# Opening of a fused encoder step: the first direct tiles and the sink column

## The chip, the cores and the metric

The kernel runs on one core of a Trainium2 chip, as one program and one launch. The metric is device time in microseconds, the median of several runs. The core has five engines that work side by side, each through its own queue in order: TensorE (PE; PEld is its weight load), VectorE (DVE), ScalarE (ACT), GpSimd (POOL) and SyncE (SP), whose queue issues nearly all transfers (DMA).

## The reference

One post-norm layer of a streaming encoder over 2048 prompt tokens and 8 x 16 sample tokens, in float32:

```python
qm, km, vm, om, ip, fp, qa, ka, va = split_in(x @ w_in)     # D_MODEL 1024 -> 2824
hm = og * head_norm(mlstm_chunkwise(qm, km, vm, logi, logf, ...))   # 4 heads x 128
qa, ka = rope(qa, pos), rope(ka, pos)
ha = band_attend(qa, ka, va, mask, attn_sinks)              # 8 q heads, 2 kv heads x 64
h = layer_norm(ALPHA * x + concat(hm, ha) @ w_out)
y = layer_norm(ALPHA * h + conv_ffn(h))                     # up 5632, causal conv of 3, silu gate, down
```

The attention's softmax has a learned sink for each head: `p = exp(s - mx) / (sum exp(s - mx) + exp(sink - mx))`, where `mx` is the maximum of the scores and the sink.

## The kernel before

Every float32 operand of a large product is split into a rounded high half (`S.copy` into float32r on ScalarE, L217 for weights, L565 for activations) and a low half (a subtraction on VectorE, L218 and L566); a product is then three matmuls, high-high, high-low and low-high.

The input projection (`i_dense`) goes over four blocks of tokens (`IBLOCKS`): block 0 holds prompt tiles 0 to 3 and the sample tile 16, the others four tiles each; a tile is 128 tokens. Five groups of 512 output columns (`NG`) are computed by a Strassen-like scheme with seven products for each group: an activation block is cut into four quarters, q = 1 to 4 (features halves 0 and 1, by token halves 0 and 1: q 1 is tiles 0 and 1 with the first half of the features, q 2 tiles 2 and 3 with the first, q 3 and q 4 the same with the second), and `x_steps` makes the sums ("t1" to "t4") and the splits (1, 2, 3, 4, 5, 6, 7 and "b12") that the products s = 1 to 7 read. `split_first` makes the sums of the weights on the way.

The gate and key/value columns (264 of them) do not go through that scheme. They are "direct" products (`i_direct`, L730): 8 slices of 128 features, three matmuls each, so 24 for a tile. Their weights come in four pieces of 264 KB (`wg`), their activations from the same splits: tiles 0 and 1 read the splits 1 (first half of the features) and 2 (second half), tiles 2 and 3 read "b12" and 3. Behind each, `i_keys` evicts the result (L738, L739 on ScalarE), turns the keys by rope (four operations on VectorE, L868 to L871) and stores them.

The order of TensorE's work is written out by hand in `i_begin`, as a list of items ("t", block, tile, ...) for directs and ("p", block, group, s) for products; `manual_schedule` keeps it. The other engines' queues are put in order by the framework's scheduler from the program and its priorities. Before the change the list begins with the directs of tiles 2 and 3, then product 1 of group 0, the direct of the sample tile, and the other products; the directs of tiles 0 and 1 stand behind block 0's last product, in front of those of tiles 2 and 3 of block 1. `advance` prefetches weights as far as free slots allow (four raw slots, eight split halves).

Beside this dense work run "chains" (`Chains`): the sample tile, the mLSTM and the attention, which are woven between the dense matmuls once `i_done` says that a block is complete. After the direct of tile 1 a counter of six items starts (`after = [6, b + 1]`); `gate_logs` then makes the logarithms of the gates on VectorE and ScalarE, and the chains may begin.

In the attention (`swa`, `scores`) the scores of four heads go into a tile `sc` with one more column, the sink. The sink column is written by GpSimd (L1297) at the beginning of `scores`; VectorE writes the masked scores and their maximum (L1307, L1310); `exps` (L1315, ScalarE) exponentiates both together with a running sum. `sc` has two buffers.

During blocks 2 and 3 `d_sums` makes sums of the down-projection's weights on VectorE (tiles `txy`, L850 to L853).

Of the kernel before, what the change touches and what calls it, by code (L numbers as in the profile page):

```python
# [204 lines left out]
class Prog:  # L205
# [131 lines left out]
    def i_begin(self):  # L337
        self.ib = [self.dps.tile([P, 512], F32, name="dps", tag="dps") for _ in range(3)]
        it = []
        nb = len(IBLOCKS)  # L340
        for b in range(nb):
            if b == 0:
                it += [("t", 0, i, -1) for i in (2, 3)]

                it += [("p", 0, 0, 1), ("t", 0, 4, -1), ("p", 0, 0, 2), ("p", 0, 1, 1), ("p", 0, 0, 7), ("p", 0, 0, 6)]
            else:
                it += [("p", b, 0, s) for s in (1, 7, 6, 2)]
            for g in range(NG):
                if b == 0:

                    it += [("p", b, g, s) for s in (6, 2)] * (g > 0) + [("p", b, g, 5)]
                    if g + 1 < NG:
                        it += [("p", b, g + 1, 1)] * (g > 0) + [("p", b, g, 4), ("p", b, g, 3), ("p", b, g + 1, 7)]
                    else:
                        it += [("p", b, g, 3), ("p", b, g, 4)]
                elif g + 1 < NG:

                    it += [("p", b, g, s) for s in (6, 7, 2)] * (g > 0)
                    it += [("p", b, g, 5), ("p", b, g + 1, 1), ("p", b, g, 3), ("p", b, g, 4)]
                else:  # L360
                    it += [("p", b, g, s) for s in (6, 7, 5, 2, 3, 4)]
            it += [("t", b, i, b) for i in (0, 1)]
            if b + 1 < nb:
                it += [("t", b + 1, i, b) for i in (2, 3)]
        self.items = it

        uq = []
        for i in it:
            if i[0] == "p":
                uq.append(i)  # L370
            elif ("g", i[3], 0) not in uq:
                uq += [("g", i[3], u) for u in range(4)]
        uq += [("o", b, h, u) for b in range(len(OBLOCKS)) for h in range(2) for u in range(4)]
        self.uq = uq
        self.wu, self.hx, self.xr = {}, {}, {}
        self.us = self.ur = 0

        self.halves = [0, 0]
        self.raws = []
        self.raw_of = {}  # L380
        self.xn = self.ny = 0
        self.hs = {}
        self.spare = False
        self.extra, self.ring, self.turn = None, 2 * WB, 0
        self.raws.append([None, False])
# [148 lines left out]
    def x_load(self, b, *qs):  # L534
        for q in qs:
            self.xr[b, q] = r = self.x_raw(q)
            self.nc.sync.dma_start(r, self.a["xq"][b][(q - 1) // 2, (q - 1) % 2])

    def x_steps(self, b, *steps):

        nc, V = self.nc, self.nc.vector
        r = lambda q: self.xr[b, q]
        for s in steps:
            if s == "t3":
                self.spare = False
                self.xt = e = self.raw_slot([P, 4, HT]) if b else [self.tp.tile([P, 4, HT], F32, name="xt", tag="qk", bufs=2), False]
                V.tensor_sub(e[0], r(4), r(2))
            elif s == "t2":

                V.tensor_add(self.xt[0], self.xt[0], r(1))  # L550
            elif s == "t4":

                V.tensor_sub(r(4), r(3), self.xt[0])
                self.xt[1] = True
            elif s == "t1":

                V.tensor_sub(r(2), r(2), r(1))
            else:
                x = self.xt[0] if s in (7, 6) else r({1: 1, 2: 3, 3: 4, "b12": 2, 5: 2, 4: 4}[s])

                self.hx[b, s] = h, l = self.x_slot(4 if s == "b12" else s)
                n = 4 if (b, s) == (0, "b12") else 1
                for i in range(n):
                    k = slice(i * 4 // n, (i + 1) * 4 // n)
                    nc.scalar.copy(h[:, k], x[:, k])  # L565
                    V.tensor_sub(l[:, k], x[:, k], h[:, k].bitcast(F32))  # L566
# [20 lines left out]
    def i_dense(self):  # L587
# [2 lines left out]
        last = NG - 1  # L590

        self.next_raw()
        self.x_load(0, 2)
        for _ in range(3):
            self.next_raw()
        self.x_load(0, 4)
        self.single_raw = self.tp.tile([P, KD, P], F32, name="xsr", tag="pth", bufs=2)
        nc.sync.dma_start(self.single_raw, a["xs"])
        self.angles = {}
        self.rope_load(IBLOCKS[0][2], 2)  # L600
        self.rope_load(NPT, 1)
        self.next_split()
        self.x_steps(0, "b12")
        for _ in range(3):
            self.next_split()
        self.x_steps(0, 3)
        self.x_single(1, 2)
        self.x_load(0, 1)
        self.next_raw()
        self.x_load(0, 3)  # L610
        self.x_steps(0, 1)
        self.advance()
        self.x_steps(0, 2, "t3", 7, "t2", 6)
        self.x_single(4)
        self.x_steps(0, "t1", 5, "t4")
        self.sb, self.trans = {}, None
# [5 lines left out]
        for item in self.items:  # L622
# [9 lines left out]
            if item[0] == "t":  # L632
                _, b, ti, e = item
                if ("g", e, 3) not in self.wu:
                    self.advance()
                if b not in self.gates:
                    self.gates[b] = self.tp.tile([P, 5, 8], F32, name="gates", tag="gates", bufs=2)
                ps = self.bank([P, 512], "pg") if ti == 4 else self.ib[ti % 2 * 2]
                yield from self.i_direct(b, ti, e, ps)
                self.i_keys(b, ti, ps)  # L640
                if ti == 1:
                    if b + 1 < nb:
                        self.x_steps(b + 1, 1, 2)
                    else:
                        self.release(4)
                    after = [6, b + 1]
                elif ti == 3 and b or ti == 4:
                    self.release(4)
                    self.x_steps(b, 4)
                    if b:  # L650
                        self.x_steps(b, 5)
                self.advance()
                continue
# [9 lines left out]
                behind = self.i_after(b, g, s)  # L663
            if (b, g, s) == (0, 0, 7):
                self.t_setup()
            if (g, s) == (1, 6):
                self.rope_load(IBLOCKS[b][0], 2)
            if g == last and b + 1 < nb:
                if s == 7:
# [45 lines left out]
                if k % 2:  # L715
                    yield 645

    def i_direct(self, b, ti, e, ps):

        mm = self.nc.tensor.matmul  # L720
        for k in range(KD):
            wh, wl = [w[:, k % 2] for w in self.wu["g", e, k // 2]]
            if ti == 4:
                xh, xl = [self.hs[1 if k < 4 else 2][:, i, k % 4] for i in range(2)]
# [546 lines left out]
    def swa(self, t):  # L1271
# [19 lines left out]
        def scores(j0):  # L1291
# [2 lines left out]
            sc = self.work("sc", [P, 4, 2 * P + 4], bufs=2)  # L1294
            mx, sm = [self.work(n, [P, 4], bufs=2) for n in ("amx", "asm")]
            w = lambda x: x.rearrange("p (k j) -> p k j", k=2)
            nc.gpsimd.tensor_copy(sc[:, :, N:N + 1].rearrange("p (k j) o -> p k (j o)", k=2), sink)  # L1297
            ps = [self.bank([P, 2, 2, P], "psc") for _ in range(2)]
            for j in range(2):
                for i, (q, k) in enumerate(((qh, self.kh), (qh, self.kl), (ql, self.kh))):  # L1300
# [7 lines left out]
                                           op0=ALU.add, op1=ALU.max, accum_out=mx[:, c:c + 1])  # L1308

            V.scalar_tensor_tensor(w(mx), w(mx), -0.125, nsink, op0=ALU.mult, op1=ALU.min)  # L1310
            return sc, mx, sm

        def exps(sc, mx, sm):
# [872 lines left out]
```

## Time and profile before

| | |
|---|---|
| runs | 2315.28, 2317.24, 2321.0 us; median 2317.24 |
| profiled execution | 2316.15 us, of which the span is 2314.3 |
| mean granted TensorE clock | 0.996 |
| TensorE busy | 2281.9 us (99%) |
| VectorE, ScalarE, GpSimd busy | 1808.1 (78%), 1269.0 (55%), 279.5 us (12%) |
| moved | 632.38 MB, mean 273 GB/s |

The rows of the profile read as follows. A row of the timeline has start, length, engine, line, operation, output and input tiles with their shapes, how often in a row, and in brackets the idle time of the engine just before, with what ended it. A row of stages has the stage, its length, the busy time of PE, PEld, DVE, ACT and POOL with counts, the granted clock, the mean busy share of the 16 DMA engines and GB/s. A row of waits has who waited for whom, the total, how often, and the longest. Lines are those of the kernel before.

### The profile page before, as it was taken

What the parts mean: (1) busy time and instruction counts of PE and PEld (TensorE: products, weight loads), DVE (VectorE), ACT (ScalarE), POOL (GpSimd) and SP (SyncE); (2) the same over time, 40 slices, a digit from 0 to 9 for tenths busy, and PEclk for the clock granted to TensorE, in tenths of its full rate; (3) what the DMA queues carried; (4) which work ended last, traced back from release to release, by engine and by line L of the source; (5) the groups of instructions that cost most, each with busy time, mean ns of one, the idle gap of its engine ahead of it and who ended that gap; (6) DMA issues with size and microseconds to landing.
All of it is one profiled execution on the core that took longest, in us unless ns stands there. A gap on an engine that the chain in (4) does not pass through costs nothing.

```text
span 2314.3 us, 39788 instructions
## 1 busy us (share of the span) xinstructions
PE 2281.9 (99%) x14293; PEld 2094.9 (91%) x14293; DVE 1808.1 (78%) x3075; ACT 1269.0 (55%) x2377; POOL 279.5 (12%) x509
## 2 busy tenths in 40 slices
PE   8999999999999999999999999999999999999998
PEld 8999989989877778999999999999999978888876
DVE  8777687787688888998788777678766786895987
ACT  5453466776766655555656555555555544444442
POOL 0001000000011212121002000013111200100200
PEclk9999999999999999999999999999999999999999
DMA  7888999999977757888778889978898776756743
GB/s 276 287 308 297 301 309 336 314 310 342 315 269 240 240 201 270 303 319 311 276 289 274 306 304 311 315 264 287 312 294 261 225 282 208 261 175 215 255 157 108
DMA packets 300166, 632.38 MB, mean 273 GB/s; under 512 B 47869, under 2 KB 141121, under 8 KB 299969
## 3 DMA queue, kind: packets, MB, share of 16 engines
q1 hardware_dynamic: 295296, 616.14, 77.9%
q0 software_dynamic: 3520, 10.56, 1.4%
q10 hardware_dynamic: 1152, 3.15, 0.4%
q8 instruction: 113, 1.85, 0.3%
q14 instruction: 85, 0.69, 0.1%
HBM read 458.11 MB, written 171.64 MB: 272 GB/s over the span
## 4 chain that ended last, share of the span: by engine, by line
PE 76%; DVE 5%; DMA 4%; issue 2%; ACT 1%; SPq 0%; POOL 0%; DVEq 0%; ACTq 0%; POOLq 0%
PE dps L1873 19%; PE fup L1873 19%; PE dps L704 7%; PE dps L2083 6%; PE fht L2083 6%; PE fup L2083 6%; PE dps L222 2%; PE dps L224 2%; PE dps L223 2%; PE ppo L1348 1%; PE psc L1303 1%; PE ppt L1342 1%; DVE w L218 1%; PE fht L1697 1%; DMA txy<-wdn 0%
## 5 line engine op out<-in xcount | busy, mean ns | idle before, releaser
L1873 PE MATMUL dps<-hh,uw 128*128 128x384 f32 (+1 forms) x1848 | 478.7, 328 | 2.0 <-DVE u L1904 2.0
L1873 PE MATMUL fup<-hh,uw 128*128 128x384 f32 (+1 forms) x1848 | 478.2, 328 | 1.5 <-ACT ua L1894 1.5
L1873 PEld LDWEIGHTS dps<-hh,uw 128*128 128x128 f32 x1848 | 330.5, 188 | 2.2 <-DVE u L1904 2.2
L1873 PEld LDWEIGHTS fup<-hh,uw 128*128 128x128 f32 x1848 | 330.0, 188 | 2.0 <-ACT ua L1894 1.9
L1930 DVE SCALAR_TENSOR_TENSOR cc<-u,cw,cc 128x768 f32<-128x768 f32 (+1 forms) x264 | 258.1, 978 | 64.9 <-ACT cc L1928 55.5
L1873 PE MATMUL fup<-hl,uw 128*128 128x384 f32 (+1 forms) x924 | 302.5, 327 | 1.7 <-DVE hl L218 1.7
L1873 PE MATMUL dps<-hl,uw 128*128 128x384 f32 (+1 forms) x924 | 302.8, 328 | 0.0
L704 PE MATMUL dps<-w,oh 128*128 128x256 f32 x1344 | 254.3, 284 | 0.7 <-DVE zev L777 0.7
L217 ACT CAST uw<-wraw 128x1024 fp32r<-128x1024 f32 x126 | 123.0, 979 | 223.8 <-PE dps L2083 120.1
L218 DVE TENSOR_TENSOR w<-wraw,w 128x1024 fp32r<-128x1024 f32 (+2 forms) x167 | 189.4, 1141 | 56.1 <-ACT w L217 48.9
L217 ACT CAST w<-wraw 128x1024 fp32r<-128x1024 f32 (+2 forms) x167 | 163.0, 985 | 107.3 <-PE dps L704 38.9
L704 PEld LDWEIGHTS dps<-w,oh 128*128 128x128 f32 x1344 | 210.5, 188 | 11.8 <-issue 8.1
L218 DVE TENSOR_TENSOR uw<-wraw,uw 128x1024 fp32r<-128x1024 f32 x126 | 142.4, 1131 | 65.7 <-ACT uw L217 65.5
L704 PE MATMUL dps<-w,ol 128*128 128x256 f32 x672 | 187.8, 279 | 0.0
L704 PE MATMUL dps<-oh,w 128*128 128x256 f32 x896 | 170.9, 285 | 6.6 <-ACT mr L1153 3.8
L1873 PEld LDWEIGHTS fup<-hl,uw 128*128 128x128 f32 x924 | 173.5, 188 | 2.4 <-DVE hl L218 2.3
L2083 PE MATMUL fup<-uw,fu 128*128 128x512 f32 x726 | 174.2, 396 | 0.6 <-DVE uw L218 0.6
L1873 PEld LDWEIGHTS dps<-hl,uw 128*128 128x128 f32 x924 | 173.8, 188 | 0.0
L2083 PEld LDWEIGHTS fup<-uw,fu 128*128 128x128 f32 x726 | 136.6, 188 | 34.1 <-DVE uw L218 1.1
L2083 PE MATMUL dps<-uw,fu 128*128 128x512 f32 x660 | 165.3, 396 | 1.1 <-DVE uw L218 1.1
L1928 ACT ACTIVATE cc<-u,cw 128x768 f32<-128x768 f32 (+1 forms) x132 | 132.2, 1002 | 57.8 <-DVE u L1910 28.5
L704 PEld LDWEIGHTS dps<-oh,w 128*128 128x128 f32 x896 | 142.2, 191 | 13.1 <-ACT mr L1153 4.1
(318 smaller groups left out, 4567.0 us busy)
## 6 DMA issues: line engine op xcount, KB each, us to landing
uw<-zw SPq DMA_DIRECT2D x176, 512.0 KB, 5.1
zw<-uw SPq DMA_DIRECT2D x88, 512.0 KB, 3.7
w<-zws SPq DMA_DIRECT2D x72, 512.0 KB, 6.2
wv<-wup SPq DMA_DIRECT2D x66, 512.0 KB, 5.0
wraw<-wi SPq DMA_DIRECT2D x65, 512.0 KB, 5.1
wraw<-zt SPq DMA_DIRECT2D x60, 512.0 KB, 4.3
wraw<-wdn SPq DMA_DIRECT2D x45, 512.0 KB, 4.3
wraw<-wo SPq DMA_DIRECT2D x40, 512.0 KB, 4.5
```

What stands on the lines that cost most here:

```text
L217: nc.scalar.copy(hi, src)
L218: nc.vector.tensor_sub(lo, src, hi.bitcast(F32))
L222: mm(out, ah, bh, start=start, stop=False)
L223: mm(out, ah, bl, start=False, stop=False)
L224: mm(out, al, bh, start=False, stop=stop)
L704: mm(o, l, r, start=s in (1, 7) and c == k == i == 0, stop=k == 3 and i == 2, skip_group_check=True)
L1303: nc.tensor.matmul(ps[kvh][:, j, :nk], q[rs, j0 + j], k[rs, sel], start=i == 0, stop=i == 2)
L1342: nc.tensor.transpose(pp[:, j * P:(j + 1) * P], scs[j // 2][:, 2 * kvh + j % 2, kt * P:(kt + 1) * P], self.ident)
L1873: mm(ps, l[:, k], r[:, k], start=s in (1, 7) and k == 0 and i == 0, stop=k == 3 and i == 2, skip_group_check=True)
L1928: S.activation(c[:, v], u[:, 2:2 + n], AF.Identity, bias=w[3], scale=w[2])
L1930: V.scalar_tensor_tensor(c[:, v], u[:, i:i + n], w[i], c[:, v], op0=ALU.mult, op1=ALU.add)
L2083: mm(ps, l[:, k, c], r[:, k], start=s in (1, 4, 7) and u == 0 and k == 0 and i == 0, stop=u == nu - 1 and k == n - 1 and i == 2, skip_grou ...
```

## The change

The directs of tiles 0 and 1 of block 0 go to the head of TensorE's list, in front of those of tiles 2 and 3: an item ("t", 0, 1) now stands for both, and goes over the first half of the features for tile 0, then tile 1, and then over the second half for both, into two accumulation banks. At the end of block 0 only the directs of tiles 2 and 3 of block 1 are left. The loads of the activations change order to match: quarter 1 (in two transfers of two slices each, between the gate pieces), 3, 2, 4, and quarter 1's split is done in four strips, where "b12" was. The counter `after` starts behind block 0's last product. The rope tables of tiles 0 and 1 are loaded at once; the splits 1 and 2 of block 1 are made at the direct of its tile 2.

The sink column is written by ScalarE, behind VectorE's maximum in the program, in place of GpSimd at the head of `scores`.

```diff
@@ i_begin
-                it += [("t", 0, i, -1) for i in (2, 3)]
+                it += [("t", 0, i, -1) for i in (1, 2, 3)]
...
-            it += [("t", b, i, b) for i in (0, 1)]
+            if b:
+                it += [("t", b, i, b) for i in (0, 1)]
@@ x_load
-            self.nc.sync.dma_start(r, self.a["xq"][b][(q - 1) // 2, (q - 1) % 2])
+            x = self.a["xq"][b][(q - 1) // 2, (q - 1) % 2]
+            n = 2 if (b, q) == (0, 1) else 1
+            for i in range(n):
+                k = slice(i * 4 // n, (i + 1) * 4 // n)
+                self.nc.sync.dma_start(r[:, k], x[:, k])
@@ x_steps
-                n = 4 if (b, s) == (0, "b12") else 1
+                n = 4 if (b, s) == (0, 1) else 1
@@ i_dense
         self.next_raw()
-        self.x_load(0, 2)
-        for _ in range(3):
+        self.x_load(0, 1)
+        self.next_raw()
+        self.x_load(0, 3)
+        for _ in range(2):
             self.next_raw()
-        self.x_load(0, 4)
+        self.x_load(0, 2, 4)
...
-        self.rope_load(IBLOCKS[0][2], 2)
+        for i in (0, 2):
+            self.rope_load(IBLOCKS[0][i], 2)
         self.rope_load(NPT, 1)
         self.next_split()
-        self.x_steps(0, "b12")
-        for _ in range(3):
+        self.x_steps(0, 1)
+        self.next_split()
+        self.x_steps(0, 2)
+        for _ in range(2):
             self.next_split()
-        self.x_steps(0, 3)
+        self.x_steps(0, "b12", 3)
         self.x_single(1, 2)
-        self.x_load(0, 1)
         self.next_raw()
-        self.x_load(0, 3)
-        self.x_steps(0, 1)
         self.advance()
-        self.x_steps(0, 2, "t3", 7, "t2", 6)
+        self.x_steps(0, "t3", 7, "t2", 6)
...
+                if b == 0 and ti == 1:
+                    for h in range(2):
+                        for i in range(2):
+                            yield from self.i_direct(b, i, e, self.ib[i * 2], (h,))
+                    self.i_keys(b, 0, self.ib[0])
+                    self.i_keys(b, 1, self.ib[2])
+                    self.advance()
+                    continue
...
+                elif (b, ti) == (1, 2):
+                    self.x_steps(b, 1, 2)
...
-            if (g, s) == (1, 6):
+            if (b, g, s) == (0, last, 4):
+                after = [6, 1]
+            if b and (g, s) == (1, 6):
                 self.rope_load(IBLOCKS[b][0], 2)
@@ i_direct
-    def i_direct(self, b, ti, e, ps):
+    def i_direct(self, b, ti, e, ps, halves=(0, 1)):
-        for k in range(KD):
+        for k in [4 * h + i for h in halves for i in range(4)]:
@@ swa, scores
-            nc.gpsimd.tensor_copy(sc[:, :, N:N + 1].rearrange("p (k j) o -> p k (j o)", k=2), sink)
...
             V.scalar_tensor_tensor(w(mx), w(mx), -0.125, nsink, op0=ALU.mult, op1=ALU.min)
+            nc.scalar.copy(sc[:, :, N:N + 1].rearrange("p (k j) o -> p k (j o)", k=2), sink)
```

## The prediction

> **What bounds the kernel now.** I read the page's first part, then the busy time by stage, then who TensorE waits for in the opening.
>
> ```profile
> span 2314.3 us, 39788 instructions
> ...
> PE 2281.9 (99%) x14293; PEld 2094.9 (91%) x14293; DVE 1808.1 (78%) x3075; ACT 1269.0 (55%) x2377; POOL 279.5 (12%) x509
> ```
>
> TensorE is busy for all but 32.4 us of the span. No edit here removes a matmul, so the whole question is where TensorE stands idle, and where it runs at half clock. The busy time by stage (length, then PE, PEld, DVE, ACT and POOL, then the granted clock, DMA share and GB/s):
>
> ```profile
> 0.00:20.00 20.00, 15.53 (x82) 13.53 (x83) 14.79 (x36) 11.55 (x23) 0.31 (x5) 0.91 0.88 331
> 20.00:40.00 20.00, 17.50 (x139) 16.54 (x138) 20.00 (x25) 11.55 (x15) 0.00 (x0) 0.99 0.64 222
> 40.00:60.00 20.00, 19.31 (x150) 18.86 (x150) 13.66 (x15) 8.74 (x13) 0.00 (x0) 0.92 0.78 268
> ```
>
> The opening, up to 60 us, holds 7.7 us of the idle time. VectorE is busy all 20.00 us of the second stage: it sets the pace there. Who TensorE's matmuls wait for in the opening (total, times, longest):
>
> ```profile
> PE dps L704 <- DVE w L218: 1.3, 2, 0.8
> PE dps L730 <- DVE w L218: 0.9, 2, 0.5
> PE dps L730 <- ACT oh L565: 0.9, 1, 0.9
> PE dps L704 <- ACT w L217: 0.8, 1, 0.8
> PE dps L730 <- DVE ol L566: 0.8, 1, 0.8
> PE dps L704 <- ACT zev L771: 0.7, 1, 0.7
> ```
>
> These are 5.4 us of gaps that earlier-ready work could fill. They also cost clock. Stages of 3.41 us, in order of time:
>
> ```profile
> 5.57:8.98 3.41, 2.53 (x14) 1.70 (x12) 3.07 (x7) 2.88 (x8) 0.00 (x0) 1.00 1.04 385
> 8.98:12.39 3.41, 1.80 (x13) 1.40 (x12) 2.88 (x4) 2.14 (x3) 0.00 (x0) 1.00 1.04 406
> 12.39:15.80 3.41, 3.41 (x18) 3.41 (x17) 3.04 (x8) 2.78 (x8) 0.00 (x0) 0.50 1.03 420
> ...
> 36.28:39.69 3.41, 1.81 (x13) 1.42 (x12) 3.41 (x6) 2.77 (x3) 0.00 (x0) 1.00 0.98 390
> 39.69:43.11 3.42, 3.42 (x19) 3.42 (x18) 3.15 (x5) 1.12 (x2) 0.00 (x0) 0.50 0.70 246
> ```
>
> Each stage with 1.6 us of idle (3.41 - 1.80 and 3.41 - 1.81) is followed by one of 3.41 us at clock 0.50; the stage with 0.9 us idle (3.41 - 2.53) is not. A half-clock stage loses 3.41 / 2 = 1.7 us. So the opening can give at most 5.4 + 2 x 1.7 = 8.8 us.
>
> **Part 1: two direct tiles leave the end of block 0.** In the built order TensorE's queue differs by 48 matmuls alone: the direct products of tiles 0 and 1 go from behind block 0's last product to the front. All four directs at that place, in two halves:
>
> ```profile
> 155.00:160.86 5.86, 5.86 (x49) 5.86 (x50) 1.00 0.78 230
> 160.86:166.72 5.86, 5.86 (x50) 5.77 (x48) 1.00 0.99 368
> ```
>
> TensorE is full in both, so the junction gets shorter by 5.86 us. That is the gain, less what the opening gets longer. The directs there also covered the split of block 1's first activations (ACT L565, DVE L566); that cover halves. The slots of those activations were held by tiles 0 and 1 themselves and now come free after block 0's last group, so I cost this at nothing; without cover it is one cast and one split.
>
> **Part 2: how long the opening becomes.** First the data. Four moments at which ScalarE begins on a landed load:
>
> ```profile
> 4.58 0.41 ACT L565 CAST oh<-xr 128x256 fp32r<-128x256 f32 x1 [2.56 <-DMA xr<-xq]
> 5.24 0.63 ACT L217 CAST w<-wraw 128x528 fp32r<-128x528 f32 x1 [0.26 <-DMA wraw<-wg]
> ...
> 8.93 1.05 ACT L565 CAST oh<-xr 128x1024 fp32r<-128x1024 f32 x1 [0.53 <-DMA xr<-xq]
> 10.27 1.14 ACT L577 CAST xs<-xsr 128x512 fp32r<-128x512 f32 x2 [0.29 <-DMA xsr<-xs]
> ```
>
> Loads go in order, an activation quarter being 512 KB and a piece of gate weights 264 KB: 512 KB are there at 4.58, 776 at 5.24, 2080 at 8.93, 2592 at 10.27. The new order is half of quarter 1, gate piece 0, the other half, piece 1, quarter 3, pieces 2 and 3, quarter 2, quarter 4: in sum 256, 520, 776, 1040, 1552, 1816, 2080, 2592 and 3104 KB. On the same curve piece 0 is there at 4.6, piece 1 at 6.0, quarter 3 at 7.4, piece 3 at 8.9, quarter 2 at 10.3 and quarter 4 at 11.6. (Estimates.) The extra issue on SP's queue costs nothing: the loads wait for bytes.
>
> Next the splits and the directs. A gate piece takes 0.63 on ScalarE and about 0.7 on VectorE (528 of the 1024 columns of a pass of 1.23, in the rows below), a quarter 1.05 and 1.2. Piece 1 is cast from 6.1 to 6.7; VectorE has done quarter 1's strips by 6.9 and its low half by 7.6. So tile 0's first half ends at 8.2 and tile 1's (12 matmuls, 1.46 us) at 9.7. Quarter 3 is split at 9.9, the low halves of pieces 2 and 3 at 10.5 and 11.1: tile 0 is whole at 11.9, tile 1 at 13.4. Quarter 4's cast stands in ScalarE's queue behind tile 0's eviction (some 0.5): it starts at 12.5, and its low half on VectorE ends at 14.75, in time for tiles 2 and 3, which run without a gap to 19.2. Idle is about 1.3 us in one stage and 0.7 in the next: a half clock there is possible, not sure.
>
> From there VectorE is the pace, as before. Its rows:
>
> ```profile
> 11.15 1.29 DVE L578 TENSOR_TENSOR xs<-xsr,xs 128x512 fp32r<-128x512 f32 x2
> ...
> 14.44 1.23 DVE L566 TENSOR_TENSOR ol<-xr,oh 128x1024 fp32r<-128x1024 f32 x1
> 15.58 1.42 DVE L218 TENSOR_TENSOR w<-wraw,w 128x256 fp32r<-128x256 f32 x4
> ...
> 31.58 0.22 DVE L868 TENSOR_TENSOR rb<-zev,ropet 128x64 f32<-128x64 f32 x1
> 31.71 0.23 DVE L869 TENSOR_TENSOR rb<-zev,ropet 128x64 f32<-128x64 f32 x1
> 31.85 1.22 DVE L566 TENSOR_TENSOR ol<-xr,oh 128x1024 fp32r<-128x1024 f32 x1
> 32.99 0.29 DVE L870 TENSOR_TENSOR zev<-zev,ropet 128x128 f32<-128x128 f32 x1
> 33.19 1.22 DVE L218 TENSOR_TENSOR w<-wraw,w 128x1024 fp32r<-128x1024 f32 x1
> ...
> 38.08 3.49 DVE L218 TENSOR_TENSOR w<-wraw,w 128x1024 fp32r<-128x1024 f32 x3
> ```
>
> Three full passes take 3.49 with the last 1.22 long, a pitch of 1.135. A tile's rope, its four operations laid between passes, takes 0.27 for the first two (31.58 to 31.85) and 0.2 for each of the others (32.99 to 33.19), 0.67. The mark is the row at 38.08: the low half of the weights of product 6 of group 0. Before, from 14.44: 18 full passes (20.4), four quarters (1.3), one sample split (0.65), two ropes (1.35): 23.7, against 23.64 measured, so the count holds. After, from 14.75 and in the built order: 15 full passes (17.0; three of the 18 are done ahead of 14.75), four quarters 1.3, three sample splits and the sample difference 2.5, five ropes 3.35, in all 24.2. The mark comes at 38.95 instead of 38.08, and its pass ends at 40.15 instead of 39.3.
>
> TensorE at that mark:
>
> ```profile
> 39.35 0.53 PE L704 MATMUL dps<-oh,w 128*128 128x256 f32 x2 [0.84 <-DVE w L218]
> ...
> 44.43 0.39 PE L704 MATMUL dps<-oh,w 128*128 128x256 f32 x1 [0.69 <-ACT zev L771]
> ```
>
> Product 6 goes on at 39.35, at half clock for the most part, and product 5 starts at 44.43 behind the eviction of its bank, a wait of 0.69 (some 0.9 from the last matmul's start). After: from 40.15, 22 matmuls at 5.86 / 48 us make 2.7, then the same 0.9: product 5 starts at 43.75 at full clock, at 45.45 with one half-clock stage. So the opening ends between 0.7 us sooner and 1.0 us later and holds 5.86 us more work: **gain 4.9 to 6.5 us**, by hand in steps of some 0.3 us. What is late next: product 1 of group 1. TensorE reaches it at about 30.7, and its weights' low half stands on VectorE behind the sums of the activations, until about 32: a new wait of 1 to 1.6 us, inside the sum already.
>
> [...] I go by the rows and take the middle of what they allow, 5.7.
>
> **Part 3: the gate logarithms move up.** With all of block 0's gates ready early, their chain on VectorE is queued at 43 to 50 us instead of 167:
>
> ```profile
> 166.00:180.00 14.00, 2.75 (x15) 0.22 (x1) 1.00 1.00 334
> ```
>
> 15 of its some 20 small operations take 2.75 us. VectorE is idle for 6.3 us of 40 to 60 (20.00 - 13.66), so I cost it at nothing; without that cover at most 2.7.
>
> **Part 4: the sink column goes from GpSimd to ScalarE.** 32 copies of 128x4. The copy before, the nearest ScalarE copy, and what the exponentials behind it wait for (total, mean, idle before and its releasers), from three views:
>
> ```profile
> L1297 POOL COPY sc<-k_sink x32: 183/190/1267, 276.3 to 826.0; 128x4 f32<-128x4 f32 x32
> ```
> ```profile
> 13.29 0.17 ACT L739 COPY gates<-dps 128x8 f32<-128x8 f32 x1
> ```
> ```profile
> L1315 ACT ACTIVATE sc<-sc,amx 128x257 f32<-128x257 f32 x120 | 59.9, 502 | 40.6 <-DVE amx L1310 37.2 <-DVE gl L995 3.3
> ```
>
> Cost 32 x 0.17 = 5.4 us of ScalarE over 550 us. The exponentials wait for VectorE's maximum and never for the copy, and in the built order the copy stands ahead of them with the slot's readers already evicted by ScalarE itself. So 0; all on the path it would be +5.4, and a gain is bounded by the one GpSimd copy of 1.27 us.
>
> **The sum.** -5.86 at the junction, -0.7 to +1.0 (0.15) in the opening, 0 and 0: -5.7. The profiled execution took 2316.15 us (span 2314.3 and 1.85 around it): 2310.4. The median of the runs is 1.1 above it, 2317.24: 2311.5. A difference under 0.3% (7.0 us: 2310.3 to 2324.2) can hardly be told from none, so this counts as no change.
>
> **Rivals.** (a) **All gaps close.** Were the opening's 5.4 us and its two half-clock stages gone, the gain is up to 8.8: 2308.4. For it: three of the six waits, those of L730, belong to the part that is rebuilt; against it: VectorE's count. It reaches further if the largest later stall goes too (TensorE's row, VectorE's wait, the stage):
>
> ```profile
> 330.30 0.58 PE L704 MATMUL dps<-oh,w 128*128 128x256 f32 x1 [3.85 <-ACT mr L1153]
> ```
> ```profile
> DVE txy L850 <- DMA txy<-wdn: 3.9, 1, 3.9
> ```
> ```profile
> 260.00:560.00 300.00, 293.10 (x2482) 273.22 (x2481) 225.95 (x609) 204.70 (x507) 25.12 (x48) 0.99 0.94 317
> ```
>
> There VectorE, held by a late load of down weights, delays an eviction: 3.85 and a half clock, 5.5 us. Without it 2317.24 - 5.7 - 5.5 = 2306.0, and with both 2302.9. (b) **The transfers become the bound, and it gets slower.** Past the junction TensorE asks for the same bytes almost 6 us earlier, while the DMA share is 0.99 in the second half of the directs and 0.94 from 260 to 560. If weights there come late by the 5.86 us of directs that covered them, the gain is lost, and a half-clock stage follows: -5.7 + 5.86 + 1.7 = +1.9, 2319; if also one more sum of down weights is caught as at 330, +7.4, 2324.6. It decides if loads at 160 to 200 us are what the casts of weights wait for. Against it: TensorE is full in the directs although the share is 0.99, and the prefetch is paced by freed slots. (c) **The copies hold ScalarE.** All 5.4 us on the path: 2317, no change. (d) That the order doesn't change as told is excluded by the built order.
>
> **How the numbers follow.** Forecast 0.48, inside 0.3%. (a) 0.36, faster by over 0.3%: the forecast stands 1.2 us from that bound. (b) 0.13, of which 0.10, with the second stall, is slower by over 0.3%. (c) 0.03, no change. So faster 0.36, slower 0.10, same 0.48 + 0.03 + 0.03 = 0.54. The range: from 2304, which leaves out the part of (a) with both its steps, 0.08, to 2320, which leaves out the slower part of (b), 0.10.
>
> **What would show it.** Right: a full TensorE at the shorter junction (two directs, 5.9 us, no new wait); product 5 of group 0 starting between 43 and 46 us; a wait for the weights' low half near 31 us; VectorE full from 15 to 40; no wait of the exponentials on ScalarE's copy. Wrong: TensorE waits for w at 150 to 200 us; product 5 at 42 (rival a) or past 48; stalls of another size from 260 to 560, where TensorE is idle 6.9 us now (300 - 293.1) and which no count of mine reaches.

## The result, and the profile after

| | median us | runs | ratio to before, 95% interval |
|---|---|---|---|
| before | 2317.05 | 22 | 1 |
| changed | 2320.44 | 22 | 1.0020 (1.0012 to 1.0027) |

The change costs 3.4 us, 0.2%. It is inside the 0.3% that counts as no change, but the time is 8.9 us above the forecast of 2311.5 and just past the end of the range. The page after, first part:

```profile
span 2320.8 us, 39712 instructions
...
PE 2281.9 (98%) x14293; PEld 2094.3 (90%) x14293; DVE 1807.6 (78%) x3075; ACT 1271.2 (55%) x2409; POOL 270.9 (12%) x477
```

TensorE does the same work (2281.9 us); its idle time went from 32.4 to 38.9 us. By stage, columns as in the prediction:

```profile
0.00:20.00 20.00, 16.27 (x95) 14.81 (x96) 12.86 (x31) 11.46 (x23) 0.31 (x5) 0.91 0.87 329
20.00:40.00 20.00, 18.62 (x157) 18.42 (x156) 19.96 (x33) 9.51 (x17) 0.00 (x0) 1.00 0.54 178
40.00:60.00 20.00, 17.07 (x141) 16.47 (x141) 18.60 (x37) 9.53 (x13) 0.00 (x0) 1.00 0.91 315
```

The first two stages gained 1.9 us of TensorE's time, the third lost 2.2 (19.31 before, though 3.1 of that stood at half clock, in the stage from 39.69). TensorE's own rows show three waits that the kernel before did not have:

```profile
51.88 0.38 PE L723 MATMUL dps<-oh,w 128*128 128x256 f32 x1 [1.46 <-DVE zev L794]
```
```profile
153.19 0.38 PE L723 MATMUL dps<-w,oh 128*128 128x256 f32 x1 [2.11 <-ACT zev L790]
163.16 0.39 PE L749 MATMUL dps<-w,ol 128*128 128x264 f32 x1 [2.40 <-DVE ol L571]
```

Together 5.97 us, as much as the 5.86 us of matmuls that left the junction. To see where time went I match TensorE's matmuls in order and subtract their starts. A half-clock stage, 3.41 us at clock 0.50, loses 1.7 us, so half the length of every such stage so far is taken from each start ("clock taken out"). Lateness against the kernel before at a matmul that stood there at the given time, in us (the column 158 is the first of the directs that stay, at 160.84; "both" is the first of its two runs):

| at (before) | 44 | 60 | 145 | 152 | 158 | 162 | 200 | 290 | 310 | 345 |
|---|---|---|---|---|---|---|---|---|---|---|
| changed | +3.3 | +4.7 | +4.7 | +7.1 | +1.2 | +3.9 | +3.9 | +4.5 | +5.8 | +4.3 |
| before, second profile | -0.9 | -0.8 | -1.9 | -1.9 | -1.9 | -1.9 | -1.9 | -1.9 | -1.8 | -2.3 |
| casts behind eviction | +3.9 | +5.2 | +4.6 | +4.6 | -0.1 | +2.9 | +2.8 | +2.8 | +3.5 | +3.4 |
| other buffer | +4.5 | +6.1 | +6.0 | +8.5 | +2.6 | +2.6 | +2.6 | +2.9 | +6.3 | +3.6 |
| both | +3.9 | +5.2 | +4.6 | +4.6 | -1.2 | -1.2 | -0.6 | -0.5 | +1.8 | -0.9 |
| both, all blocks | +3.6 | +4.7 | +5.7 | +5.7 | -0.1 | -0.1 | +0.2 | +0.2 | +1.8 | +1.4 |

The row "changed" reads: +3.3 until product 5 (5.86 us more work, 2.6 us of it in former idle time), +1.4 by the wait at 52 us, +2.4 by the one at 153, -5.9 at the junction, +2.7 by the one at 163. So 3.9 us late at 200 us, against a saving that was meant to be there. Two profiles of the kernel before differ by 2 us up to 345 us and by more further on (the second one is at +1.1 at 2200 us), so a single pair is read to no better than that. The waits themselves recur: 1.8 to 2.4 us for the one at 153 us and 2.1 to 2.5 for the one at 163, in all profiles of the kernels that leave their causes alone.

Each span is split in the same way: what the clock took (span x (1 - mean clock)) and the rest. Means over the runs: before 8.9 to 9.5 and 2305.6 to 2305.9 in the four later sets of 23 to 35 runs, changed 8.4 and 2310.5. The clock's share is nearly the same; the rest grew by 4.7 us.

### The profile page after: what moved, and what is told of

Its sections match the earlier page's. It is cut to its first block, busy times and chain, and to the rows that moved or that the text cites. A ratio compares the mean times of both kernels' runs of the same rounds, so it can differ in the third digit from the quotient of the medians.

```text
span 2320.8 us, 39712 instructions
## 1 busy us (share of the span) xinstructions
PE 2281.9 (98%) x14293; PEld 2094.3 (90%) x14293; DVE 1807.6 (78%) x3075; ACT 1271.2 (55%) x2409; POOL 270.9 (12%) x477
## 5 line engine op out<-in xcount | busy, mean ns | idle before, releaser
L723 PE MATMUL dps<-w,oh 128*128 128x256 f32 x1344 | 255.0, 284 | 2.8 <-ACT zev L790 2.4
L723 PEld LDWEIGHTS dps<-w,oh 128*128 128x128 f32 x1344 | 210.6, 188 | 14.6 <-issue 8.1
L723 PE MATMUL dps<-w,ol 128*128 128x256 f32 x672 | 187.8, 279 | 0.0
L723 PE MATMUL dps<-oh,w 128*128 128x256 f32 x896 | 169.3, 284 | 6.5 <-ACT mr L1172 2.2
L723 PEld LDWEIGHTS dps<-oh,w 128*128 128x128 f32 x896 | 141.1, 190 | 12.6 <-issue 4.1
```

The lines of the kernel that those rows point to most:

```text
L723: mm(o, l, r, start=s in (1, 7) and c == k == i == 0, stop=k == 3 and i == 2, skip_group_check=True)
```

## The experiments

**The kernel before, a second profile.**

> The kernel before, looked at a second time, for its TensorE clock: in its first profile stages of half clock stand at 12.4 and 39.7 us. Theory (a stage is a fixed 3.41 us of a clock whose phase to the program is another in every execution, and whether a stage is halved hangs on how much idle time falls into the one before it): the stages stand at other places or are missing, by another offset on the 3.41 us grid, and product 5 of the first group starts up to 1.7 us earlier than the 44.43 us of the first profile if the one near 39.7 us is missing. Rival (the stages belong to the kernel's own stalls and come at the same places every time): both are there again within 0.3 us, and product 5 starts at 44.1 to 44.8 us.

2317.22 us. Stages around the two places (length, PE, PEld, DVE, ACT, POOL, clock, DMA share, GB/s):

```profile
6.41:9.82 3.41, 1.87 (x11) 1.44 (x11) 2.71 (x6) 2.78 (x5) 0.00 (x0) 1.00 1.04 394
9.82:13.23 3.41, 2.90 (x11) 2.60 (x12) 3.12 (x4) 1.14 (x3) 0.00 (x0) 0.50 1.03 416
...
37.12:40.54 3.42, 1.81 (x14) 1.42 (x13) 3.42 (x6) 2.84 (x3) 0.00 (x0) 1.00 1.00 396
40.54:43.95 3.41, 3.41 (x18) 3.41 (x18) 3.08 (x5) 1.06 (x2) 0.00 (x0) 0.50 0.71 263
```

Neither side wholly: the grid of 3.41 us stands elsewhere (9.82 and 40.54, not 12.39 and 39.69), yet the stage with the stalls near 38 us, 1.61 us of idle TensorE (3.42 - 1.81), is again followed by one at clock 0.50, and product 5 starts at 45.21. The stage from 13.23 to 16.65 is at half clock too, so that this opening has three such stages where the first profile has two. The loss near 40 us belongs to the old opening; its exact place does not.

**The sink column back on GpSimd.** The copy stands at the head of the scores again:

```diff
+            nc.gpsimd.tensor_copy(sc[:, :, N:N + 1].rearrange(...), sink)
...
-            nc.scalar.copy(sc[:, :, N:N + 1].rearrange(...), sink)
```

> The changed kernel with one part undone: the copy of the sink column is again GpSimd's, at the head of the scores; the opening, the direct tiles and the gate logarithms stay as changed. Theory (the sink copy is free; the loss sits in the opening, in VectorE's queue near 52 us and in the waits near 153 and 163 us): the time stays within 1.5 us of the changed kernel, the offsets of TensorE's matmuls before 330 us are the same to 0.3 us, and the waits of 1.5 us (52 us), 2.1 us (153 us) and 2.4 us (163 us) are still there. Rival (ScalarE's copies hold back its evictions in the chains): 3 to 6 us faster than the changed kernel, nearly all of it won between 300 and 860 us.

2321.01 us, ratio 1.0018 (1.0007 to 1.0029): as the changed kernel. (TensorE's lateness agrees less well than the 0.3 us expected: +3.2 at 290 us, where the changed kernel has +4.5.) In the changed kernel's view by line, the exponentials' waits (total us, times) name VectorE alone. A copy on their own engine could not be named there; what it costs is read from the time of this run:

```profile
L1334 ACT ACTIVATE sc<-sc,amx x128: 388/498/517, 320.1 to 850.0; 128x257 f32<-128x257 f32 x120, 128x129 f32<-128x129 f32 x8
...
its engine sat idle before it (us, times) until:
  DVE amx L1328: 37.4, 20
  DVE gl L1014: 3.2, 1
```

This run is also the changed kernel's opening and junction once more, on another phase of the clock's grid. Stages at the junction, its two waits of 2.1 us mainly inside the first and the third:

```profile
149.69:153.11 3.42, 1.58 (x13) 1.58 (x14) 1.99 (x4) 2.28 (x4) 0.13 (x1) 1.00 0.53 181
153.11:156.52 3.41, 3.41 (x18) 3.41 (x18) 0.65 (x1) 0.71 (x2) 0.00 (x0) 0.50 0.92 321
159.93:163.35 3.42, 1.33 (x11) 1.12 (x10) 3.42 (x4) 1.60 (x3) 0.00 (x0) 1.00 0.84 255
163.35:166.76 3.41, 3.41 (x18) 3.41 (x17) 2.29 (x3) 1.05 (x1) 0.00 (x0) 0.50 0.99 332
```

Here the stages with the waits have 1.84 and 2.09 us of idle TensorE (3.42 - 1.58 and 3.42 - 1.33), and a half-clock stage follows each; in the changed kernel's own profile the same waits straddle the grid, a stage has 1.49 us of idle at most (158.84 to 162.25), and none follows.

**The gate logarithms late.**

```diff
-                    self.logs_of(after[1] - 1)
+                    with self.tc.issue_after(self.last_add) if after[1] == 1 else nullcontext():
+                        self.logs_of(after[1] - 1)
```

> The changed kernel, with VectorE's part of block 0's gate logarithms queued behind VectorE's last sum of block 0, so that nothing of them runs near 50 us. Theory (they stand among the opening's splits in VectorE's queue and cost TensorE the wait of 1.46 us at 51.9 us): that wait is gone, TensorE stands 1.2 to 1.5 us earlier at 60 us, and the whole is 1 to 2 us faster than the changed kernel, less what the junction near 160 us gives back, up to 0.7 us, since three small operations now stand there. Rival (VectorE would be late there without them, because its splits carry the opening's delay): the wait keeps more than 1 us and TensorE stands within 0.4 us of where it stood.

2322.27 us, 1.0017 (1.0004 to 1.0031). My theory fell: TensorE still waits 1.30 us at 51.82, and at 60 us it stands where it stood (+4.6, not +4.7). VectorE in the changed kernel, then in this one:

```profile
46.10 0.19 DVE L1000 TENSOR_TENSOR g<-gates,k_gb 128x40 f32<-128x40 f32 x1
...
48.85 1.23 DVE L509 TENSOR_TENSOR wraw<-wraw 128x1024 f32<-128x1024 f32 x1
50.00 1.22 DVE L218 TENSOR_TENSOR w<-wraw,w 128x1024 fp32r<-128x1024 f32 x1
51.13 0.69 DVE L794 SCALAR_TENSOR_TENSOR zev<-dps,zev 128x512 f32<-128x512 f32 x1
```
```profile
46.74 1.23 DVE L506 TENSOR_TENSOR wraw<-wraw 128x1024 f32<-128x1024 f32 x1 [0.50 <-DMA wraw<-wi]
48.80 1.23 DVE L509 TENSOR_TENSOR wraw<-wraw 128x1024 f32<-128x1024 f32 x1 [0.83 <-DMA wraw<-wi]
49.94 1.22 DVE L218 TENSOR_TENSOR w<-wraw,w 128x1024 fp32r<-128x1024 f32 x1
51.08 0.69 DVE L795 SCALAR_TENSOR_TENSOR zev<-dps,zev 128x512 f32<-128x512 f32 x1
```

The logarithms only filled time in which VectorE would have waited for loads. What stands in front of the eviction L794 is the weights' sum L509: it starts at 48.85 with the logarithms, and at 48.80 without them, when its load lands. Before, the sum stood behind the eviction (L775 at 48.12, L508 at 48.73).

**The logarithms late and the weights' sum behind the eviction.** Beside the edit above:

```diff
+        if u == ("p", 0, 1, 6) and not self.out05:
+            return False
...
+            if (b, g, s) == (0, 0, 5):
+                self.out05 = True
+                behind = self.u4_add
```

> The changed kernel, with block 0's gate logarithms late as before in this study, and also VectorE's sum for the weights of product 6 of group 1 queued behind the first scaled sum that empties a bank of group 0. With the logarithms alone moved, that sum stood in front and waited 0.8 us for its load at 48.8 us. Theory (VectorE's order is the cause: what waits for a load stands ahead of what TensorE waits for): the wait of 1.3 to 1.5 us near 51.8 us falls under 0.5 us and TensorE stands 0.9 to 1.4 us earlier at 60 us than in the changed kernel, clock taken out. Rival (the scaled sum is late by the weights' low half at 50.0 us in front of it, or by its own inputs): over 1 us of the wait stays.

2319.14 us, 1.0014 (1.0004 to 1.0025). The wait is down to 0.56 us, and TensorE loses 0.6 us from 44 to 60 us in place of 1.4: the order was the cause. (At 60 us itself it is only 0.3 us earlier, +4.4 for +4.7, less than expected: this run was later at 44 us already.) Yet at 200 us it is at +3.3, where the sink run is at +3.2: what this wins is waited for again before the junction.

**The casts behind the eviction.** ScalarE before the wait at 153 us in the changed kernel, then in the kernel of this edit:

```profile
152.02 0.63 ACT L217 CAST w<-wraw 128x528 fp32r<-128x528 f32 x1 [3.42 <-DMA wraw<-wg]
152.55 0.58 ACT L790 COPY zev<-dps 128x512 f32<-128x512 f32 x1
```
```profile
148.41 0.58 ACT L796 COPY zev<-dps 128x512 f32<-128x512 f32 x1
150.65 1.36 ACT L217 CAST w<-wraw 128x528 fp32r<-128x528 f32 x2 [1.66 <-DMA wraw<-wg]
```
```diff
+        if u[:2] == ("g", 0) and u[2] >= 1 and not self.out5:
+            return False
...
+            if (b, g, s) == (0, last, 5):
+                self.out5 = True
+                behind = self.u4_copy
```

> The changed kernel, with ScalarE's casts of the second to fourth quarters of the gate and key weights for block 1 queued behind the eviction of product 5 of block 0's last group, and nothing else moved: ScalarE no longer stands 3.42 us before a load with that eviction behind it. Theory (head of line: the eviction was ready and the wait for the load in front of it cost TensorE 2.11 us at 153.2 us): that wait falls under 0.3 us, TensorE stands 1.8 to 2.1 us earlier at 158 us. What follows it, the low half of the split at 162 us, moves with it, so the whole is 1 to 2.1 us faster. Rival (the load itself, late in the queue, is the bound, and the casts only show it): the wait goes, but the direct tiles near 160 us wait for their weights by the same 2 us, and the whole is within 0.5 us of the changed kernel.

The wait at 153 us is gone, TensorE is level with the kernel before at 158 us (-0.1; changed +1.2). But the whole is 2321.89 us, 1.0019 (1.0004 to 1.0033). Who TensorE waits for from 140 to 170 us:

```profile
PE dps L755 <- DVE ol L573: 2.7, 1, 2.7
PE dps L755 <- ACT oh L572: 1.0, 1, 1.0
```

The next wait grows from 2.4 to 3.7 us in two parts, since its split cannot start before the last product ends, and a half-clock stage follows it (161.1 us). Neither theory nor rival as written: the direct tiles wait, but for their split, not for the weights.

**Another buffer for the split.**

```diff
-                self.hx[b, s] = h, l = self.x_slot(4 if s == "b12" else s)
+                self.hx[b, s] = h, l = self.x_slot((4 if s == "b12" else s) if b != 1 else {"b12": 2, 2: 4, 4: 2}.get(s, s))
```

> The changed kernel, with block 1's split of the second quarter (read by the direct tiles 2 and 3) put in the buffer that product 2 has left, and product 2's own split in the one that the last product leaves: the same instructions, one buffer that comes free two products earlier. Theory (the wait of 2.40 us at 163.2 us is this split, which could not start before the last product had left its buffer, and the 48 matmuls that used to cover it are gone): the split's low half is done before 158 us, the wait falls under 0.4 us, and the whole is 1.5 to 2.5 us faster. Rival (VectorE has as much to do there whatever the buffer, and another of its results is late in place of this one): the wait only changes its name, to the weights or to an eviction, over 1.5 us of it stays, and the whole is within 0.7 us.

2319.86 us, 1.0011 (0.9999 to 1.0022). The wait at 163 us is gone: from 158 to 162 us TensorE loses 0.0 where it lost 2.7. So that split was late because its buffer was held by the last product. The whole gains little: 0.6 us by the medians; with the clock's share taken out 2.1 us (2308.3 for 2310.5; 95%: 0.0 to 4.3). The wait at 153 us is still there (2.4 us), and block 2 has new ones, told below.

**Both edits at the junction**, twice.

> The changed kernel with both changes near the junction: the casts of the gate and key weights behind product 5's eviction, and the split of the second quarter in the earlier buffer. Theory (two waits of 2.1 and 2.4 us, each with its own cause, in a row on TensorE's path): both are gone, and TensorE stands 4 to 5 us earlier at 200 us than in the changed kernel, clock taken out, about level with the kernel before or up to 1.5 us ahead of it; the whole 2.5 to 5 us under the changed kernel. Rival (there is one store of slack, and what one edit wins the other's wait takes): under 3 us at 200 us, and a new wait over 1 us between 150 and 170 us. A second rival for the whole: the recurrence and attention chains from 290 us on run by their own loads and take back most of it, so that under 1.5 us is left at the end.

> The changed kernel with both edits near the junction once more, so that its time against the kernel before rests on two sets of runs. Theory (both waits were real and nothing takes their place): again 2311 to 2316 us in the median, under the kernel before by 1 to 5 us, TensorE again 4 to 5.5 us earlier at 200 us than in the changed kernel with the clock taken out, and no stage of half clock between 145 and 170 us. Rival (the first set was lucky in its stages of half clock): 2317 us or more.

2313.77 us, 0.9986 (0.9973 to 0.9998), and 2314.96 us, 0.9992 (0.9981 to 1.0004). From 140 to 170 us this is all that is left in the first run, and nothing in the second:

```profile
PE dps L729 <- ACT dps L804: 0.4, 1, 0.4
```

TensorE stands 4.5 us earlier at 200 us than in the changed kernel (-0.6 for +3.9), 5.4 in the second run. The rest of the span falls from 2310.5 to 2305.7 and 2305.9, the clock's share from 8.4 to 6.7 and 7.2: two waits less, and fewer half-clock stages, none of them from 145 to 170 us. Alone the casts' edit won nothing in the whole and the buffer 0.6 us by the medians, together they win 6 us. At 200 us the two alone stand 1.1 and 1.3 us earlier than the changed kernel, both together 4.5 and 5.4.

**The same with the sink column on GpSimd.**

> As the run with both edits near the junction, and the sink column copied by GpSimd at the head of the scores again. Theory (the copy is free on either engine): within 1.5 us of that run. Rival (ScalarE's copies hold back evictions in the chains, which was hidden while other waits ruled): 2 us or more faster, won between 290 and 860 us.

2316.28 us, 0.9999 (0.9989 to 1.0008): 1.3 and 2.5 us above the two runs with ScalarE's copy, not faster (2.5 is more than the 1.5 us expected, but the intervals overlap). The copy shows no cost on ScalarE.

**All four edits**: logarithms, weights' sum, casts, buffer.

> The changed kernel with four edits: gate logarithms late, the weights' sum of group 1 behind the first scaled sum, the casts of the gate and key weights behind product 5's eviction, the split of the second quarter in the earlier buffer. Theory (the waits stand in a row on TensorE's path and add up): the waits at 52, 153 and 162 us are all under 0.6 us, TensorE stands 5 to 6.5 us earlier at 200 us than in the changed kernel with the clock taken out, and the whole is 0 to 1.5 us under the run with the two edits of the junction. Rival (what is won at 52 us is waited for again before 150 us, as it was when the two edits there ran alone): the same as the run with two edits within 1 us.

2312.97 us, 0.9988 (0.9976 to 1.0000). TensorE is 1.6 us further ahead at 200 us (-2.2 for -0.6), but the times do not tell the two kernels apart.

**The exchange of buffers in all later blocks.** With block 1 alone, block 2's split takes the buffer that direct tiles 0 and 1 of block 1 still read. Waits of 290 to 306 us in the run with the other buffer alone:

```profile
PE dps L749 <- ACT oh L570: 2.8, 1, 2.8
PE dps L749 <- DVE ol L571: 1.9, 1, 1.9
```
```diff
+                self.hx[b, s] = h, l = self.x_slot({"b12": 2, 2: 4, 4: 2}.get(s, s) if b else 4 if s == "b12" else s)
```

> As the run with both edits near the junction, but the exchange of the two buffers holds for all later blocks, not for block 1 alone. With block 1 alone, block 2's split of the second quarter takes the buffer that block 1's direct tiles 0 and 1 still read: two new waits (2.8 and 1.9 us in one run, 1.0 and 1.9 us in the other) and stages of half clock stand near 297 us. Theory (the same fault as at 162 us, made anew one block later by the edit): both waits near 295 us fall under 0.6 us in sum, and TensorE stands 2 to 5 us earlier at 310 us, clock taken out, than in the two runs with block 1 alone; some of it is lost again at 330 us, where a late load of down weights holds VectorE, so that the whole is 0 to 3 us faster. Rival (the waits there come from late casts on ScalarE, as the changed kernel's own 1.26 us at 299.9 us on an eviction): over 2 us of them stays.

> The four edits together (logarithms late, sum of weights behind the scaled sum, casts behind product 5's eviction, buffers), with the exchange of buffers in all later blocks. Theory (each wait has its own cause and the parts add): the waits at 52, 153, 162 and 297 us are all small, TensorE stands 5 to 7 us earlier at 290 us than in the changed kernel, clock taken out, and the whole is 2308 to 2314 us, under the kernel before with an interval that leaves out 1. Rival (the stall at 330 us, held by a load, takes back what comes before it): 2313 to 2317 us, with a stall over 3 us at 330 us.

2312.59 us with the casts' edit and 2312.38 us with all four, both 0.9980 (0.9969 to 0.9992). The same waits in the first of them:

```profile
PE dps L755 <- ACT gates L764: 1.6, 1, 1.6
```

The splits' waits are gone, one on an eviction stays (1.3 us in the changed kernel, none before). The clock's share is 5.8 us in both, the lowest of all, and the rest 2304.5 and 2304.6. These two are 4 us faster than the kernel before and 8 us faster than the changed one; the edits at 52 us add nothing to the whole. Against the runs with the exchange in block 1 alone the gain is not shown: the intervals overlap, TensorE is at +1.8 at 310 us where those two runs have +1.8 and +3.5 (2 to 5 us had been expected), and what block 2 wins is lost again at 330 us. The stall there, in which the prediction saw VectorE held by a late load, is 0.6 to 0.8 us in the five runs with block 1 alone and 2.6 and 2.9 us in these two; at 345 us they are at +1.4 and, with all four edits, -1.3, for -0.9, +1.0 and, with all four edits, -2.0.

**Two at the opening.**

```diff
+                    with self.tc.issue_after(self.q4_cast):
+                        self.i_keys(b, 0, self.ib[0])
```

> The changed kernel, with ScalarE's eviction of tile 0 queued behind its cast of the fourth quarter, in place of ahead of it; the scheduler orders what follows anew. In the changed kernel that cast waits for TensorE to end tile 0 (14.17 us) though its quarter has landed before, and VectorE idles 1.93 us in front of the cast's low half, at the head of the pass that sets the opening's length. Theory (the pass starts when that low half can): it starts 1 to 1.9 us earlier, and product 5 of group 0 starts 0.8 to 1.9 us earlier than 44.3 us (46.01 us less the stage of half clock). Rival (the fourth quarter lands only then, or the new order costs what the start wins): within 0.5 us or later.

2319.06 us, 1.0014 (1.0001 to 1.0027). ScalarE on quarter 4, in the changed kernel and in this one:

```profile
14.50 1.06 ACT L570 CAST oh<-xr 128x1024 fp32r<-128x1024 f32 x1
```
```profile
12.15 1.05 ACT L570 CAST oh<-xr 128x1024 fp32r<-128x1024 f32 x1 [0.19 <-DMA xr<-xq]
```

The quarter lands at 12.15 and is cast 2.35 us sooner, and VectorE is through with its low half at 14.38 in place of 16.73, but the new order behind it loses this: product 5 starts at 45.47. The nine kernels with the changed opening's own order and no half clock in it have 44.60 to 45.53. Inconclusive on the cast, since the order changed with it.

```diff
-            n = 2 if (b, q) == (0, 1) else 1
+            n = 1
```

> The changed kernel with the first quarter of the features loaded in one transfer, not in two halves with a gate piece between; the scheduler orders what follows anew. Theory (two halves and a piece in turn bring the first cast 0.36 us forward and the later pieces back, and the opening is set by VectorE's pass, not by the first cast): tile 0 ends within 0.5 us of where it did, product 5 starts at 44.4 to 45.4 us (no stage of half clock in the opening), no difference beyond 1 us in the whole. Rival (the halves make the later pieces late by over 1 us, and that carries through): product 5 starts 1 us or more earlier, and the whole is over 1 us faster.

2319.11 us, 1.0009 (0.9999 to 1.0018). Product 5 starts at 44.55, the early end of those nine, so one whole load is no worse than two halves. The halves alone are not isolated: the order changed here too (quarter 4 is cast at 12.04, in front of tile 0's eviction, as in the run above). The whole is 1.3 us lower by the medians, a little more than the 1 us expected, and the intervals overlap.

## Why the prediction was wrong

**The 48 matmuls: right.** From 152 to 158 us the lateness falls by 5.9 us (changed), 5.8 (both edits).

**"That cover halves ... I cost this at nothing": the step that failed most.** I looked at the slots of the two splits that tiles 0 and 1 had held. The one that mattered is the split for tiles 2 and 3, whose buffer the last product holds; tiles 0 and 1 used to run meanwhile. Its row is the wait of 2.40 us. ScalarE's cast for it waits for the last product (L723), and VectorE's low half comes behind two other operations:

```profile
159.14 1.05 ACT L570 CAST oh<-xr 128x1024 fp32r<-128x1024 f32 x1 [0.35 <-PE dps L723]
...
161.89 1.22 DVE L571 TENSOR_TENSOR ol<-xr,oh 128x1024 fp32r<-128x1024 f32 x1
```

I had named the price, "one cast and one split" (1.05 and 1.2 us by the prediction's own rows), and then not charged it. The other buffer shows it.

**The wait at 153 us: missing from the sum.** In ScalarE's queue a cast stood 3.42 us before a load, and the eviction for TensorE's next product behind it (152.02 and 152.55). The kernel before had waits for the same loads, the longer one with the eviction in front:

```profile
146.22 0.64 ACT L217 CAST w<-wraw 128x528 fp32r<-128x528 f32 x1 [1.35 <-DMA wraw<-wg]
146.75 0.58 ACT L771 COPY zev<-dps 128x512 f32<-128x512 f32 x1
149.39 1.27 ACT L217 CAST w<-wraw 128x528 fp32r<-128x528 f32 x2 [2.05 <-DMA wraw<-wg]
```

The casts' edit shows the cause. Rival (b) spoke of casts of weights that wait for loads, behind the junction, and its 2319 is near, but by luck: TensorE waits for no weights there, and the wait at 153 us went when the order did, with a cast still waiting 1.66 us for its load. Why the changed program was given the other order of cast and eviction no run shows.

**The two together** are 5.1 us of lateness (2.4 and 2.7). Mending both wins 6 us, and 7.9 with the buffers exchanged in all blocks (2320.44 to 2312.59), which is 1.1 us above the forecast. But these kernels do not come there by the way that was forecast. Of the 5.7 us of forecast gain, 3.1 were TensorE's path: 5.86 less 2.7, since product 5 was to start at 43.75 at full clock, for 44.43 less two half-clock stages, 41.0. The other 2.6 were clock. The path came out 3.9 us later at 200 us, so 7 us are missing there: 5.1 at these two waits, 1.4 at 52 us and 0.6 in the opening (+3.3 for +2.7). With both waits mended the rest of the span (2305.7 and 2305.9) is no more than level with the kernel before; what is won on that kernel is clock. From 200 us on the changed kernel loses 0.8 us more (4.7 for 3.9), which I leave open.

**The opening: size nearly right, reason half right.** VectorE's count of 24.2 us to the mark was measured at 24.5 (16.73 to 41.27), the new wait near 31 to 32 us is 1.38 at 34.38. The start was 2 us late (16.73 for 14.75): quarter 1's second half is cast at 6.44 and piece 1 at 7.52, for 5.24 and 6.1 by the byte curve, and a half-clock stage stood at 8.65. In the twelve profiles with this opening's order the two casts come at 5.4 to 6.7 and at 6.2 to 7.8 us, so loads in the same order land over 1 us apart from one execution to the next, and the curve of one profile is no better than that. The stage:

```profile
5.24:8.65 3.41, 1.96 (x10) 1.17 (x8) 2.27 (x5) 1.91 (x5) 0.00 (x0) 1.00 0.98 371
8.65:12.06 3.41, 3.11 (x14) 3.12 (x15) 2.47 (x4) 2.83 (x4) 0.00 (x0) 0.50 1.02 416
```

Product 5 starts at 46.01 here, at 45.98 and 46.07 in the two other profiles with that stage, and at 44.60 to 45.53 in the nine without: against 44.43 and 45.21 in the two profiles of before, a change of -0.6 to +1.6 us where I took +0.15. That is 0.9 to 1.8 us later than forecast without such a stage (43.75) and 0.5 to 0.6 later with one (45.45). The longest gap in 5.24:8.65 is 1.04 us, the idle time in sum 1.45 (3.41 - 1.96), and a half-clock stage follows.

**The clock: a term too large.** I credited the two half-clock stages of the old opening as won, but for one that might stay (2.6 us in the middle), and put none elsewhere. They moved: no half clock near 40 us in any of the 14 profiles with the new opening, but a stage between 150 and 167 us in six of the eight that keep a wait of over 2 us at the junction, the changed kernel's own not among the six. The mean loss is hardly less, 8.4 us for 8.9 to 9.5: 0.5 to 1.1 us won.

**The gate logarithms: nothing, as said**, though VectorE's order at 52 us was not foreseen (1.46 us of wait, without weight in the whole). **The sink copy: nothing, as said.**

## What to carry to other kernels

Before work is moved away from a seam, list what it was covering: every buffer that comes free there, and who fills it next. In each engine's queue, look for a cast that waits for a load in front of an eviction that another engine waits for. And mend neighbouring waits together: one alone may win nothing, since the next one takes the time, as it did when the casts alone were moved (2.4 us of wait became 3.7).

## What the runs showed of the hardware

The profiles show the clock granted in stages of 3.41 us, on a grid whose place against the program differs from one execution to the next: in the first profile of the kernel before, half-clock stages start at 12.39 and 39.69 us, 27.30 apart, which is eight stages; in the second, the first starts at 9.82. Whether a stage was at half clock went, for the most part, with the idle time in sum of the stage before it. In the 16 profiles of this study, from 4.5 to 2250 us, all 31 stages with 1.96 us or more of idle TensorE were followed by half clock (in the first profile of the kernel before and in the changed kernel's five, with 1.98 to 3.38), of the 31 with 1.45 to 1.95 us eleven were, and of the some 10,450 with less six, five of which were at half clock themselves. The sum is not all of it: of the 31 in the middle, six of the seven whose idle time came in several gaps of at most 1.3 us were followed by half clock, but only five of the 24 with one gap of 1.45 us or more. Why is open. The wait at 153 us cost 2.1 us in the changed kernel's profile, where the grid parts it (0.95 and 1.16 us of idle in two stages), and by an estimate 3.8 (2.1 and 1.7) with the sink column on GpSimd, where 1.84 us of idle fall into one stage. In the 22 runs of the changed kernel (2314.46 to 2328.82 us) span and mean clock have a correlation of -0.8.

A first load of 256 KB was cast from at 3.96 to 4.33 us in 13 profiles, one of 512 KB at 4.12, 4.14 and 4.58 in three: half the bytes brought nothing that stands out of the spread.
